# Layer 1 of a two-layer trunk: the stage from the projection to the experts in a fixed order, with a pairwise ranking of the experts

## The chip, the cores and the metric

One NeuronCore of a Trainium2 chip runs the whole program. The metric is device microseconds of one execution; the time of a kernel is the median of its runs. The profile is that of one execution, taken by the hardware profiler. TensorE (PE), VectorE (DVE), ScalarE (ACT), GpSimd (POOL) and the DMA queue of SyncE (SP) run side by side and wait for each other by semaphores; each takes its instructions in order.

## The reference

512 tokens of width 1024 pass two layers. Each layer has a mixer, a cross-attention into 256 memory tokens and a mixture of 16 experts; after each of the three the sum with the scaled input is normalised. The stage that is edited begins in the output projection `wo` of layer 1's cross-attention and ends in its experts:

```
x = layer_norm(ALPHA * x + memory_cross_attention(x, mem, xq, xkv, xo), ln2_g, ln2_b)
x = layer_norm(ALPHA * x + grouped_moe(x, router_w, router_bias, e_gate, e_up, e_down), ln3_g, ln3_b)

# grouped_moe
scores = softmax(xt @ router_w)                  # 512 x 16
biased = scores + router_bias
grouped = biased.reshape(-1, 4, 4)               # 4 groups of 4 experts
group_score = sum(top_k(grouped, 2))             # best two of each group
g_sel = argmax(group_score)                      # one group for each token
_, local_idx = top_k(in_group, 2)                # two experts of it
weights = sel / sum(sel)                         # by the scores without bias
for e in range(16):
    he = silu(xt @ w_gate[e]) * (xt @ w_up[e])
    y += combine[:, e:e+1] * (he @ w_down[e])
```

## The kernel before

The tokens lie in four tiles `X[0]` to `X[3]` of 128 rows. Every matmul of the trunk is done in three (`mm3`, L281): both operands are split into a high and a low part. All weights come as one stream `W` (class `Stream`, L108) of pieces of 512 KB: SP loads a piece into a `raw` buffer (`pump`, L129), ScalarE makes its high part (`whi`, L153) and VectorE the low one (`wlo`, L156) in `prepare`; `take` gives the pieces to a matmul and splits `look` pieces further on (3, in the experts 4), `last_ahead` bounds that. `depth` pieces are loaded ahead of the one that is split (21 in the experts of layer 1, so piece i is loaded as piece i - 22 is split); before the experts `pump` loads up to 26 pieces past the split ones. A pool of 44 buffers holds pieces, split parts and other tiles.

`project_and_norm` (L388) does the projection `wo`: its first 512 columns for all tiles together (`rows_together`), then the second 512 columns tile by tile (`rows_of_tile`, 24 matmuls of 512 columns for each tile). For each tile VectorE adds the residual (L339), takes the statistics (L352, L357) and applies the norm (L381, L386), with the power on GpSimd (L346). `r.tile_in` (L868) follows for each tile: a transfer of the tile to DRAM from ScalarE's queue (L870), 8 transposes (L875), the copy of the transposes (L879, for the last half tile L877 on VectorE), the scaling by ALPHA in place and its transfer (L880, L881), and the logits of the 16 experts (16 matmuls of 16 columns, L885; evacuated by L886). The steps of the tiles are advanced one behind the other; the logits of tile t follow the matmuls of tile t + 1. After the last tile's logits `route` (L890) chooses for all 512 tokens at once: maximum, exponential, sum, division, bias (L901 to L908), then the two best of each group by maximum, comparison and removal, and the best group (L914 to L935), giving a mask `mk` of 0 and 1. `cnt` (L941, L942) counts with small matmuls which place of an expert's list a token has (`pos`, L943).

`moe` (L1051) makes the lists: `index` (L1007) compares `pos` of an expert with the slots (`one_hot`, L973), sums token numbers by matmuls (L996), converts them (`set_rows`, L1001 and L1002), and GpSimd gathers the tokens' rows from DRAM (`fetch`, L1033). `weights` (L947) and `largest` (L961) come in between. `turned(0)` transposes and splits the gathered rows (L268, L258, L259). `experts` (L1091) then runs for each expert: gate of the next expert, down, up of the next expert, 24 matmuls of 512 columns each, with 12 weight pieces; the product of gate and up is L1112, its transposes are L1121, the split of these is `hT`.

Order: outside of `tc.manual_schedule` the compiler orders the instructions of each engine by priority and readiness; inside it the instructions of TensorE, ScalarE and VectorE keep the order in which the code emits them. Before, only `experts` stood in such a block. Layer 0 runs the same functions, and fills the choosing time of TensorE with the keys of layer 1's memory (`kfill`).

## Time and profile before

| | us |
|---|---|
| median of three runs | 1307.77 |
| lowest and highest | 1305.97, 1308.52 |
| the profiled execution, own time | 1310.58 |
| its span, first to last instruction | 1308.4 |
| mean granted TensorE clock | 0.979 of full |
| share of the span busy: TensorE, VectorE, ScalarE, GpSimd | 95%, 75%, 59%, 13% |

A line of a timeline has the start in us from the span's start, the length in us, the engine, the source line, the operation, output <- input with their shapes and the number of merged instructions; in brackets stands how long the engine was idle before, and what ended that. Of merged instructions the length is that of all together. In a table of stretches each engine has its busy time and, in brackets, its instructions; then come the granted TensorE clock, the busy share of the DMA engines and what they moved in GB/s.

### The profile page before, as it was taken

How to read it: one execution, taken by the hardware profiler on the slowest of the kernel's cores; microseconds unless marked ns; L12 is line 12 of the kernel's file. 1: busy time of each engine (PE TensorE's matmuls, PEld its weight loads, DVE VectorE, ACT ScalarE, POOL GpSimd, SP SyncE). 2: the span in 40 equal slices, each digit the busy share in tenths (PEclk: the TensorE clock that was granted, in tenths of full speed). 3: DMA queues.
4: the chain of work that ended last, by engine and by line, in shares of the span. 5: the costliest groups of instructions: out<-in, count | busy, mean ns of one | idle time of the engine just before them, and what ended most of it. 6: DMA issues, size and time to landing. Idle time of an engine off the chain costs nothing. (4 is left out here: it accounts for less than half of the span.)

```text
span 1308.4 us, 18639 instructions
## 1 busy us (share of the span) xinstructions
PE 1242.6 (95%) x6680; PEld 1042.5 (80%) x6680; DVE 982.5 (75%) x1482; ACT 768.8 (59%) x1143; POOL 170.4 (13%) x171
## 2 busy tenths in 40 slices
PE   8999999999989999999997979999978999999996
PEld 6877989888888888787775968888866888888873
DVE  4785746474769999998885586738567999999975
ACT  4765613363348888878763433227226878778873
POOL 2010001000101101111011130100011111111113
PEclk9999999999999999999998999999988999999997
DMA  9113422329549999999997333105754999999993
GB/s 320 53 49 113 164 79 81 97 89 324 192 151 325 340 339 341 328 342 345 345 355 238 130 103 122 65 33 185 263 197 145 334 365 336 345 348 346 351 324 134
DMA packets 133666, 298.81 MB, mean 228 GB/s; under 512 B 13819, under 2 KB 15883, under 8 KB 133568
## 3 DMA queue, kind: packets, MB, share of 16 engines
q1 hardware_dynamic: 118528, 260.08, 55.8%
q0 software_dynamic: 12160, 27.01, 7.5%
q10 hardware_dynamic: 2880, 10.49, 2.1%
q8 instruction: 53, 0.87, 0.3%
q14 instruction: 45, 0.37, 0.1%
HBM read 287.40 MB, written 26.74 MB: 240 GB/s over the span
## 5 line engine op out<-in xcount | busy, mean ns | idle before, releaser
L156 DVE TENSOR_TENSOR wlo<-raw,whi 128x1024 fp32r<-128x1024 f32 x486 | 572.1, 1221 | 94.1 <-ACT whi L153 70.0
L153 ACT ACTIVATE whi<-raw 128x1024 fp32r<-128x1024 f32 x488 | 490.8, 1059 | 70.6 <-PE mm L283 26.3
L282 PE MATMUL mm<-whi,xgTh 128*128 128x512 f32 x512 | 207.9, 406 | 0.0
L284 PE MATMUL mm<-whi,xgTl 128*128 128x512 f32 x512 | 201.0, 393 | 0.0
L283 PE MATMUL mm<-wlo,xgTh 128*128 128x512 f32 x512 | 200.2, 391 | 0.0
L284 PEld LDWEIGHTS mm<-whi,xgTl 128*128 128x128 f32 x512 | 96.4, 188 | 21.6 <-DVE xgTl L259 0.2
L1038 POOL DMA_INDIRECT l_y<-ye,r_idx x31 | 49.8, 1606 | 473.3 <-ACT ye L1155 209.4
L283 PEld LDWEIGHTS mm<-wlo,xgTh 128*128 128x128 f32 x512 | 97.0, 189 | 18.0
L282 PEld LDWEIGHTS mm<-whi,xgTh 128*128 128x128 f32 x512 | 96.8, 189 | 17.7 <-ACT xgTh L258 0.2
L284 PE MATMUL mm<-whi,hT 128*128 128x512 f32 x256 | 103.5, 404 | 3.3 <-DVE hT L259 3.3
L282 PE MATMUL mm<-whi,hT 128*128 128x512 f32 x256 | 103.7, 405 | 1.4 <-ACT hT L258 1.4
L283 PE MATMUL mm<-wlo,hT 128*128 128x512 f32 x256 | 101.4, 396 | 0.7 <-DVE wlo L156 0.7
L258 ACT ACTIVATE xgTh<-tp 128x512 fp32r<-128x512 f32 x64 | 38.2, 602 | 67.2 <-PE tp L268 67.2
L268 PE MATMUL tp<-ident,x 128*128 128x128 f32 x384 | 58.0, 285 | 17.4 <-DMA x<-in_x_dram 6.3
L268 PEld LDWEIGHTS tp<-ident,x 128*128 128x128 f32 x384 | 48.7, 147 | 27.7 <-issue 12.2
L346 POOL TENSOR_TENSOR ln_rs<-ln_rs,half_neg 128x1 f32<-128x1 f32 x24 | 31.7, 1320 | 286.2 <-DVE ln_rs L345 286.2
L284 PEld LDWEIGHTS mm<-whi,hT 128*128 128x128 f32 x256 | 48.7, 190 | 21.2 <-DVE hT L259 11.3
L258 ACT ACTIVATE x1Th<-tp 128x256 fp32r<-128x256 f32 x32 | 12.1, 383 | 86.5 <-PE tp L268 75.9
L282 PE MATMUL mm<-x1Th,whi 128*128 128x256 f32 (+1 forms) x192 | 60.7, 321 | 0.7 <-DVE xqTl L259 0.7
L283 PE MATMUL mm<-x1Tl,whi 128*128 128x256 f32 (+1 forms) x192 | 60.9, 318 | 0.0
L284 PE MATMUL mm<-x1Th,wlo 128*128 128x256 f32 (+1 forms) x192 | 60.9, 318 | 0.0
L283 PEld LDWEIGHTS mm<-wlo,hT 128*128 128x128 f32 x256 | 48.8, 191 | 11.1 <-DVE wlo L156 1.8
(328 smaller groups left out, 2547.7 us busy)
## 6 DMA issues: line engine op xcount, KB each, us to landing
raw<-in_l_e_gate_dram SPq DMA_DIRECT2D x128, 512.0 KB, 5.5
raw<-in_l_e_up_dram SPq DMA_DIRECT2D x128, 512.0 KB, 6.6
raw<-in_l_e_down_dram SPq DMA_DIRECT2D x128, 512.0 KB, 5.6
raw<-in_l_xkv_dram SPq DMA_DIRECT2D x32, 512.0 KB, 5.4
raw<-in_l_w_in_dram SPq DMA_DIRECT2D x22, 512.0 KB, 6.4
raw<-in_l_w_out_dram SPq DMA_DIRECT2D x16, 512.0 KB, 4.2
raw<-in_l_xq_dram SPq DMA_DIRECT2D x16, 512.0 KB, 4.5
raw<-in_l_xo_dram SPq DMA_DIRECT2D x16, 512.0 KB, 3.7
```

The source lines that it names most:

```text
L153: first = act(hi, raw, AF.Copy)
L156: self.last_split = [first, eng.tensor_sub(lo, raw, hi.bitcast(F32))]
L258: act(hi, src, AF.Copy)
L268: transpose(tp[:, j], rows(c0 + j), ident)
L282: mm(ps, sh, mh, start=first, stop=False)
L283: mm(ps, sh, ml, start=False, stop=False)
L284: return mm(ps, sl, mh, start=False, stop=last)
L346: nc.gpsimd.tensor_tensor(rs[:, 1:2], rs[:, 0:1], half_neg[:, 0:1], op=ALU.pow)
L1038: return nc.gpsimd.indirect_dma_start(out=self.y_dram[:], out_offset=bass.IndirectOffsetOnAxis(ap=idx, axis=0), in_=ye, in_offset=None, bo ...
```

## The change

In layer 1 the part from the second half of the projection to the end of the experts stands in one `manual_schedule` block, so its order on TensorE, ScalarE and VectorE is the order of the code. A new function `project_and_route` writes this order: the logits of a tile stand inside the matmuls of a later tile (after the fourth of eight chunks); the scaling of a tile is put off by two tiles; the first three tiles choose their experts in one step, and then the last tile alone, its logits read from PSUM; a weight piece of the first expert is split between the two. `last_ahead` holds the splitting of the experts' weights back until then: one piece is split there and one after `weights`, where three were split during the projection before. `moe` of layer 1 makes the lists of experts 0 and 1, then the weights, then the transposes. `warm_up` issues matmuls whose result nobody reads: 8, 8 and 9.

For both layers `choose` ranks the experts of a group by comparing each with each: greater, or equal and earlier (`tri`), counted by a sum; `G` is four groups times the tiles; the mask is "fewer than two above" in the best group.

```
+WARM = (8, 8, 9)
...
-    def rows_of_tile(xT, w, n, t):
+    def rows_of_tile(xT, w, n, t, jobs={}):
...
+            if k in jobs:
+                next(jobs[k], None)
...
+    def project_and_route(xT, key, ln, r, warm):
+        end = W.span[(key, 1)][1]
+        W.last_ahead = end
+        w = W.take((key, 1))
+        tiles = [r.tile_in(t) for t in range(NT)]
+        three, one = r.choose(slice(0, NT - 1)), r.choose(slice(NT - 1, NT))
+        for t in range(NT):
+            ln.residual(t, 1, rows_of_tile(xT, w, 512, t, {SPLIT_AT: tiles[t - 2]} if t > 1 else {}))
+            if t == NT - 1:
+                next(tiles[2])
+            ln.norm(t)
+            if t > 1:
+                r.scaled(t - 2)
+            if t == 1:
+                next(tiles[0])
+            elif t == 2:
+                next(tiles[1])
+        next(tiles[2], None)
+        warm(WARM[0])
+        steps(three, 2)
+        r.scaled(2)
+        next(tiles[3])
+        W.prepare(end + 1)
+        next(tiles[3], None)
+        warm(WARM[1])
+        steps(one, 2)
+        r.scaled(3)
+        r.count()
+        W.last_ahead = 1 << 30
...
+    def warm_up(n, oh=None):
+        ps = mmt("warm")
+        x = tb.tok.rearrange("p t e c -> p (t e c)") if oh is None else oh.rearrange("p t s -> p (t s)")
+        for _ in range(n):
+            mm(ps[:, :x.shape[-1]], tb.upto, x, start=True, stop=True)
...
+        def choose(self, ts):
+            lg = self.last_lg if ts.start else self.lg[:, ts]
...
             red(mx, lg, axis=AX.X, op=ALU.max)
-            tt(lg, lg, over(mx), op=ALU.subtract)
-            ex, bi = w16("exp"), w16("biased")
-            act(ex, lg, AF.Exp)
+            tt(ex, lg, over(mx), op=ALU.subtract)
+            act(ex, ex, AF.Exp)
             red(total, ex, axis=AX.X, op=ALU.add)
             vec.reciprocal(rt, total)
             tt(bi, ex, over(rt), op=ALU.mult)
             tt(bi, bi, tb.b[:, None, :].to_broadcast(T3), op=ALU.add)
...
+            S = [128, G, 4, 4]
...
+            tt(above[:, :, :, 4:], other, own, op=ALU.is_equal)
+            tt(above[:, :, :, 4:], above[:, :, :, 4:], tb.tri[:, None].to_broadcast(S), op=ALU.mult)
+            tt(above[:, :, :, :4], other, own, op=ALU.is_gt)
+            red(flat(rank), above, axis=AX.X, op=ALU.add)
+            vec.scalar_tensor_tensor(top, rank, 1.5, bi, op0=ALU.is_lt, op1=ALU.mult)
+            red(gs.rearrange("p t g -> p (t g)"), flat(top), axis=AX.X, op=ALU.add)
             red(gm, gs, axis=AX.X, op=ALU.max)
             tt(gs, gs, bc(gm), op=ALU.is_equal)
+            tt(gs, gs, tb.desc[:, None, :4].to_broadcast([128, n, 4]), op=ALU.mult)
             red(gf, gs, axis=AX.X, op=ALU.max)
             tt(gs, gs, bc(gf), op=ALU.is_equal)
+            vec.scalar_tensor_tensor(flat(mk), flat(rank), 1.5, each, op0=ALU.is_lt, op1=ALU.mult)
...
+            for e in range(2):
+                ohs.append(r.one_hot(r.pos[:, :, e:e + 1]))
+                r.sums(ps[e][:, 0], ohs[e], tb.tok[:, :, e], 0, 2)
+                r.set_rows(r.idx[:, e:e + 1], ps[e])
+                W.after = fetch(e)
+            warm(WARM[2], ohs[1])
+            r.weights()
+            W.prepare(W.split + 1)
+            xT = turned(0)
+            for e in range(2):
+                r.sums(ps[e][:, 0], ohs[e], tb.tok[:, :, e], 2, 5)
+            r.largest()
+            for e in range(2):
+                r.set_weights(r.ws[:, e:e + 1], ps[e])
             ln = experts(r, xT, groups, fetch, turn_part, turned, keep)
...
+            rows_together(oT, W.take((p + "xo", 0)), 512, lambda t, ps: ln.residual(t, 0, ps))
+            with tc.manual_schedule(engines=THREE):
+                project_and_route(oT, p + "xo", ln, r, warm_up)
+                W.depth, W.look = MOE_DEPTH[p], MOE_LOOK
+                ln = moe(r, None, True, warm_up)
```

## Rows read from the trace of the kernel before

**Rows 1.** Page, part 1: busy time, share of the span, instructions.

```profile
PE 1242.6 (95%) x6680; PEld 1042.5 (80%) x6680; DVE 982.5 (75%) x1482; ACT 768.8 (59%) x1143; POOL 170.4 (13%) x171
```

**Rows 2.** Table of stretches, layer 0's first expert and then layer 1.

```profile
385.00:390.00 5.00, 3.63 (x19) 3.63 (x20) 4.86 (x6) 5.00 (x7) 0.00 (x0) 0.66 0.01 6
970.00:985.00 15.00, 5.02 (x46) 4.61 (x46) 9.09 (x47) 1.97 (x4) 1.69 (x2) 0.50 0.28 110
990.66:1004.37 13.71, 13.71 (x63) 11.15 (x62) 11.98 (x15) 12.33 (x15) 1.22 (x1) 0.90 0.36 101
995.00:1005.00 10.00, 10.00 (x53) 8.19 (x52) 8.53 (x13) 8.32 (x10) 1.22 (x1) 1.00 0.56 163
1020.00:1250.00 230.00, 229.78 (x1118) 187.38 (x1117) 216.06 (x235) 186.58 (x229) 33.40 (x24) 1.00 0.98 347
```

**Rows 3.** Timeline of VectorE, norm of the last tile.

```profile
963.43 0.69 DVE L339 SCALAR_TENSOR_TENSOR x<-x,mm 128x512 f32<-128x512 f32 x1 [3.30 <-PE mm L284]
...
966.92 1.28 DVE L386 SCALAR_TENSOR_TENSOR x<-x,ln_rs,ln_b 128x1024 f32<-128x1024 f32 x1 [0.44 <-POOL ln_rs L346]
```

**Rows 4.** Timeline of TensorE, logits and transposes after the projection.

```profile
963.24 1.85 PE L885 MATMUL lg<-router_w,rxT 128*128 128x16 f32 x16
964.94 1.07 PE L875 MATMUL tp<-ident,x 128*128 128x128 f32 x8
...
970.64 3.60 PE L885 MATMUL lg<-router_w,rxT 128*128 128x16 f32 x16 [1.28 <-ACT rxT L879]
```

**Rows 5.** Timeline of VectorE, the choice and the first index.

```profile
974.49 0.22 DVE L901 TENSOR_REDUCE r_max<-r_lg 128x4 f32<-128x64 f32 x1 [4.41 <-ACT r_lg L886]
...
976.34 0.22 DVE L914 TENSOR_REDUCE rg_m<-r_biased 128x16 f32<-128x64 f32 x1
976.59 0.22 DVE L915 TENSOR_TENSOR r_d<-r_biased,rg_m 128x64 f32<-128x64 f32 x1
...
978.13 0.17 DVE L924 TENSOR_TENSOR rg_gs<-rg_m,rg_m 128x16 f32<-128x16 f32 x1
...
979.59 0.22 DVE L935 TENSOR_TENSOR r_mk<-r_s,rg_gs 128x64 bf16<-128x64 f32 x1
...
980.59 1.29 DVE L973 TENSOR_TENSOR r_oh<-slot,r_pos 128x512 bf16<-128x512 f32 x2
...
982.00 0.15 DVE L1002 TENSOR_SCALAR r_idx<-r_row 128x1 int32<-128x1 f32 x1
```

**Rows 6.** Timeline of GpSimd, the gather of expert 0.

```profile
983.01 1.12 POOL L1033 DMA_INDIRECT x<-l_x,r_idx  x1 [16.13 <-DVE tokv L957]
```

**Rows 7.** Timeline of TensorE, transposes and gate of expert 0, transposes of h.

```profile
987.36 1.94 PE L268 MATMUL tp<-ident,x 128*128 128x128 f32 x8 [3.39 <-DMA x<-l_x,r_idx]
989.13 0.79 PE L282 MATMUL mm<-whi,xgTh 128*128 128x512 f32 x1
...
993.96 0.39 PE L282 MATMUL mm<-whi,xgTh 128*128 128x512 f32 x1
...
996.68 0.25 PE L996 MATMUL idx<-tokv,r_oh 128*128 128x5 bf16 x4
...
1005.98 0.60 PE L1121 MATMUL tp<-ident,h 128*128 128x128 f32 x4
```

**Rows 8.** Timeline of VectorE, second half of the gathered rows, first product.

```profile
989.97 0.69 DVE L259 TENSOR_TENSOR xgTl<-tp,xgTh 128x512 fp32r<-128x512 f32 x1 [0.16 <-ACT xgTh L258]
...
1004.37 0.68 DVE L1112 TENSOR_TENSOR h<-h,mm 128x512 f32<-128x512 f32 x1
```

**Rows 9.** Timeline of layer 0, transposes and split of expert 0's rows.

```profile
383.63 1.06 PE L268 MATMUL tp<-ident,x 128*128 128x128 f32 x8 [1.88 <-DMA x<-l_x,r_idx]
...
384.92 1.29 DVE L259 TENSOR_TENSOR xgTl<-tp,xgTh 128x512 fp32r<-128x512 f32 x2 [3.91 <-ACT xgTh L258]
```

**Rows 10.** Timeline of VectorE at the end of the experts.

```profile
1266.98 2.59 DVE L156 TENSOR_TENSOR wlo<-raw,whi 128x1024 fp32r<-128x1024 f32 x2 [0.82 <-ACT whi L153]
...
1273.35 0.69 DVE L1112 TENSOR_TENSOR h<-h,mm 128x512 f32<-128x512 f32 x1 [1.69 <-PE mm L284]
```

99 lines of the change are left out of this document (50 added, 49 removed).

## The prediction

> **What bounds the kernel now.** I read the busy line of the page first: TensorE works in 95% of the span, so a change to some 50 us in the middle can move little unless it empties a hole [rows 1]. Then the table of stretches, cut at the borders of the stage that is edited [rows 2]. It shows three regimes. From 970 to 985 TensorE works 5.02 of 15 us at a granted clock of 0.50, the 1.2 GHz level; this is the hole in which the experts are chosen. From 995 to 1005 it is full, and the DMA is not (0.56). From 1020 to 1250 TensorE (229.78 of 230), VectorE (216.06) and the DMA (0.98 of its time) are all at their limit together. So the time won in the hole must pass a second gate: the first expert, where VectorE is the tight engine, and a third: the stream of weights.
>
> The timelines of the hole give its chain. VectorE gets the last tile's second half of the projection at 963.43, after waiting 3.30 us for TensorE, and ends the tile's norm 4.77 us later, at 966.92 + 1.28 = 968.20 [rows 3]; the logits start at 970.64 and take 3.60 us at the low clock, where those of tile 1 took 1.7 [rows 4]; the choice runs on VectorE from 974.49 to 979.59 + 0.22 = 979.81, the index is ready at 982.15 [rows 5], the gather is issued at 983.01 [rows 6], and the first transpose on its rows starts at 987.36 [rows 7]. The split of these rows is finished at 989.97 + 0.69 = 990.66 [rows 8]; I call this point T.
>
> **Part 1: the order up to the last tile's norm.** The logits of tile 1, 1.70 us (963.24 to 964.94, [rows 4]), used to follow the last tile's matmuls; now they stand inside them, after the fourth of eight chunks. VectorE waits for TensorE there [rows 3], so the last tile's half ends at 963.43 + 1.70 = 965.13 and its norm, the same 4.77 us, at 969.90. I call this R. It is a loss of 1.70 us. The transposes and logits of tile 2 (some 3.3 us from 964.94 on) still fit before R. Gone from this stretch are three early splits of expert weights, on VectorE 1.2 us each, and the scaling of a tile right behind its transfer, which is put off on ScalarE by two tiles. As TensorE sets the pace here, I give both nothing; were that cover gone, the splits would be worth up to 3.6.
>
> **Part 2: two choices in place of one.** No row has the pairwise operations, so I size them by elements: 16 elements take 0.17 us and 64 take 0.22 [rows 5], 512 take 0.69 [rows 3], which is 0.153 + 0.00105 per element (1.22 for the 1024 of a split); a dependent operation follows 0.03 after the end (976.34 to 976.59 with 0.22 busy). The part from the maximum to the biased scores took 974.49 to 976.34 = 1.85 us for four tiles, with the exponential on ScalarE inside; by size I take 1.75 for three tiles, 1.55 for one. The ranking part has 12 operations. Three tiles: 3 of 192 elements, one overlapped (1.07), a sum over 384 (0.59), 3 of 48 (0.72), 5 small (1.0) = 3.4. One tile: 0.68 + 0.32 + 0.6 + 0.95 = 2.55. So three tiles end at R + 5.15. VectorE's order is now fixed: behind them stands the split of one weight piece, 1.2 us, to R + 6.3, and only then the last tile's choice, 4.1 us. Its logits are ready earlier if the clock holds: before, they began 970.64 - 968.20 = 2.4 after R; now the exponential of the three tiles, a scaling and its transfer's issue stand ahead of the copy on ScalarE, and I take 3.1, so logits of 1.7 end at R + 4.85. At the low clock (3.6) they end at R + 6.7. So the mask is complete at R + 10.4 = 980.3, against 979.81: the chain from R became 1.2 us shorter, but R is 1.7 later. For the unseen sizes: the ranking parts have 1550 elements in all, 1.6 us, so a cost of only the fixed part gives 1.6 less for both choices and twice the cost per element 1.6 more; I keep the fitted value, since the rows are tensor operations of the same engine, but keep both ends for the range.
>
> **Part 3: index and gather.** Nine of the ten counting matmuls no longer need the last mask, and weights are no longer mixed in before the positions: the one-hot of expert 0 starts 0.5 us after the mask (before: 980.59, 0.78 after). The index of expert 0 no longer stands behind the second one-hot; 1.40 in place of 1.56. Index at 982.2 against 982.15; issue and landing as before, 0.86 and 4.35 [rows 5 to 7]. Rows of expert 0 at 987.4: no change.
>
> **Part 4: the warm matmuls.** They are 8, 8 and 9, of 320 columns and 512 in the last; at 0.227 us for 512 columns at the high clock (the gate's last 12 matmuls take 993.96 to 996.68, [rows 7]) about 1.1, 1.1 and 2 us, all in waits of TensorE. Before, the clock fell to the 1.2 GHz level by 970, some 6.5 us after the last tile's matmuls, though logits and transposes ran meanwhile [rows 2, 4]; in layer 0 it fell sooner: the key matmuls end 1.88 us before 383.63, then only transposes run, and the stretch 385:390 has 0.66 [rows 2, 9]. So I trust the warm matmuls for the logits of the last tile and for the transposes of expert 0, less for the gate. With the clock held, transposes to T take 2.58 us as in layer 0 (383.63 to 384.92 + 1.29 = 386.21, [rows 9]) instead of 987.36 to 990.66 = 3.30: T is 0.7 us earlier. The gate before paid for the low clock too: its 24 matmuls went from 989.13 to 996.68 = 7.55; at the later pace, 0.227 each, they take 5.46, so 2.1 us were lost [rows 7]. The Trainium skill ("TensorE: Matmul & The Clock Gate", section "Why this matters for your kernels") advises to leave no long idle gaps between bursts so that the clock stays up; by that advice alone these 2.1 us would be won as well.
>
> **Part 5: why the gate's share is not won.** At T only two pieces of expert 0's weights are split, before three. VectorE from T = 990.66 to expert 0's product at 1004.37 had 11.98 us of work in 13.7 [rows 2, 8]. Now come one more split (1.2), the one-hot of expert 2 (0.6, before ahead of T), and the largest count and two weight sums (0.5): 14.3 in all, so the product starts 0.6 later from T and, with T 0.7 earlier, about 0.1 earlier than before. TensorE had 0.9 us of slack against it there (product done 1005.05, transposes of h at 1005.98, [rows 7, 8]), so it gains up to 0.9 for a moment and then waits for the low half of hT, which VectorE makes after the product: I let it keep 0.5. From there on the period is the same.
>
> **Part 6: the stream of weights.** A piece is loaded when the piece 22 before it is split. 27 pieces lie ready at the gate instead of 29; the two more (524 KB each, 1.5 us at the 347 GB/s of 1020:1250) fall at 995 to 998, where the DMA is used to 0.56 [rows 2], so I cost them at nothing. If that cover were gone, 3.0 us would come at the end, where VectorE splits the last two pieces of an up matrix from 1266.98 to 1269.57 after a wait, and TensorE, done with that matrix at 1273.3, started on its last piece (6 matmuls, 1.37 us) at 1271.95: 2.4 us are left [rows 10].
>
> **Part 7: layer 0** gets the new choice for four tiles at once: by the same sizes 3.72 us against the 976.34 to 979.81 = 3.47 of the same lines in layer 1 [rows 5]; TensorE waits there 1.88 us for the gathered rows [rows 9], so this is on the path: +0.2 (-1.4 to +1.8 by the same two ends).
>
> **Sum:** -0.5 + 0.2 = -0.3 us on the profiled execution, whose span is 1308.4 and whose own time 1310.58 is 2.8 us above the median of the runs shown, 1307.77. Carried to the median: 1307.5.
>
> **Rivals.** *The clock decides, VectorE does not* (faster). If the extra VectorE work fits into TensorE's faster first expert, the 0.7 and the 2.1 us of part 4 come through whole, and with half of the early split (0.6), should it slip out of the chain: 1307.77 - 2.8 - 0.6 + 0.2 = 1304.6. For it: rows show the low clock all through the hole; TensorE, not VectorE, is the full engine in 995:1005 [rows 2]. Against it: part 5's count. This is also where the skill's advice leads.
> *The clock falls in spite of the warm matmuls and the fixed order makes everyone wait* (slower). The last logits at 3.6 us put the last choice at R + 6.7 (+0.4), transposes stay at 3.3 (+0.7), and a gate at the low clock takes TensorE's slack against the first product (+0.5): 1.6 later than in my sum, 1309.1; with the pairwise operations at their upper end (+1.6, layer 0 +1.6) 1312.3. It decides from the point where the logits end after R + 6.3, when VectorE would be free.
> *The stream sets the end*: the hole shrinks, but the last pieces come no earlier; TensorE waits for them. As 2.4 us are left there, this gives 1307.8, or up to 1309 if part 6's cover is gone.
> *The change doesn't do what it says*: the three early choices cannot start before VectorE has finished the last tile's norm, so "first" buys only their 5.15 us beside the logits; that is in my sum.
>
> **How the numbers follow.** A measurement of this kernel tells about 0.2% (2.6 us) from no change. Forecast 0.44 and stream 0.07 are within 0.2%. Clock decides: 0.28, all of it faster. Slow rival: 0.21; its plain price stays within 0.2%, and I give two thirds, 0.14, to the bounds that carry it past 1310.4, and 0.07 to no change. Range: the forecast with both ends of the pairwise cost is 1304.3 to 1310.7; with the faster case and the plain slow one inside it is 1304.0 to 1310.8. Faster 0.28, same 0.58, slower 0.14.
>
> **What would show it.** Right: the norm of the last tile ends near 970 in the new trace, the last mask near 980, the gather is issued within 0.7 us of 983; the stretch from T to the first product is longer than before and without waits of VectorE, while TensorE shows a wait for h of about a microsecond after the first gate. Wrong: a wait of VectorE for the last tile's logits (the slow rival), a first product 2 us or more earlier (the fast one), a longer wait of ScalarE for the last pieces (the stream). I would be most wrong if the pairwise operations cost other than by their elements, or if the order before the hole moves TensorE's work differently than by 1.70.

## The result and the profile after

The changed kernel is slower: 1316.28 us (1314.87 to 1318.12) against 1307.35 of the kernel before in the same series, a ratio of 1.0070 with a 95% interval of 1.0052 to 1.0087, or +9.2 us. A second series of it gave +4.1 us (ratio 1.0031, interval 1.0011 to 1.0051). Both lie on the side that had a chance of 0.14, and the first median lies outside the range of 1304.0 to 1310.8. The profiled execution of the changed kernel took 1315.8 us, its span is 1314.1.

The busy line of the page says little: 5.3 us more of TensorE in a span that is 5.7 us longer than that of [rows 1].

```profile
PE 1247.9 (95%) x6705; PEld 1043.5 (79%) x6705; DVE 986.0 (75%) x1486; ACT 771.1 (59%) x1144; POOL 170.3 (13%) x171
```

The table of stretches of the changed kernel is to be read beside [rows 2]. Its columns are the stretch and its length, the busy time of TensorE, its weight loads, VectorE, ScalarE and GpSimd, then the granted clock, the DMA's share and GB/s. The layer-1 stage lies some 3.5 us later here, so 975:990 stands for 970:985, and 994.14:1007.93 (point T to the first product) for 990.66:1004.37.

```profile
385.00:390.00 5.00, 3.32 (x18) 3.08 (x17) 4.01 (x5) 4.78 (x7) 0.00 (x0) 0.56 0.06 20
975.00:990.00 15.00, 9.54 (x50) 6.39 (x51) 11.79 (x49) 4.45 (x7) 2.13 (x2) 0.54 0.44 150
994.14:1007.93 13.79, 13.79 (x70) 11.27 (x69) 13.72 (x21) 13.38 (x16) 1.22 (x1) 1.00 0.52 159
1020.00:1250.00 230.00, 228.51 (x1109) 185.69 (x1108) 213.33 (x235) 185.23 (x226) 36.05 (x26) 1.00 0.96 336
```

The hole in which experts are chosen is fuller (TensorE 9.54 of 15 us instead of 5.02, more than half of it warm matmuls), and the clock is at its upper level from T on. But from T to the first product VectorE works 13.72 of 13.79 us, so nothing got shorter there; and the stream in 1020:1250 is slower, 336 GB/s instead of 347.

The timeline of VectorE in the changed kernel, from the second half of the last tile to the first product of layer 1, is to be read beside [rows 3, 5, 8]:

```profile
968.74 0.69 DVE L342 SCALAR_TENSOR_TENSOR x<-x,mm 128x512 f32<-128x512 f32 x1 [3.44 <-PE mm L285]
...
972.22 1.29 DVE L389 SCALAR_TENSOR_TENSOR x<-x,ln_rs,ln_b 128x1024 f32<-128x1024 f32 x1 [0.44 <-POOL ln_rs L349]
...
975.12 0.36 DVE L973 TENSOR_TENSOR above<-r_biased 128x192 f32<-128x192 f32 x1
...
978.25 0.21 DVE L990 SCALAR_TENSOR_TENSOR r_mk<-r_rank,rg_gs 128x48 bf16<-128x48 f32 x1
978.38 1.22 DVE L157 TENSOR_TENSOR wlo<-raw,whi 128x1024 fp32r<-128x1024 f32 x1
980.26 0.17 DVE L961 TENSOR_REDUCE r_max<-lg 128x1 f32<-128x16 f32 x1 [0.67 <-PE lg L937]
...
984.11 0.17 DVE L990 SCALAR_TENSOR_TENSOR r_mk<-r_rank,rg_gs 128x16 bf16<-128x16 f32 x1
...
984.80 0.69 DVE L1028 TENSOR_TENSOR r_oh<-slot,r_pos 128x512 bf16<-128x512 f32 x1
...
1004.52 3.49 DVE L157 TENSOR_TENSOR wlo<-raw,whi 128x1024 fp32r<-128x1024 f32 x3
1007.93 0.68 DVE L1185 TENSOR_TENSOR h<-h,mm 128x512 f32<-128x512 f32 x1
```

The norm of the last tile ends at 973.51; three tiles have chosen 4.95 us later, at 978.46. The first product follows VectorE's weight splits without a gap, while the gate and up matmuls that it needs are over at 1006.0: VectorE, and not TensorE, sets its time. The new wait of VectorE in the choice, 0.67 us ahead of 980.26, is for the last tile's logits. The timeline of TensorE has them, in the place of the last row of [rows 4], at the low clock all the same:

```profile
976.63 3.60 PE L937 MATMUL lg<-router_w,rxT 128*128 128x16 f32 x16 [1.97 <-ACT rxT L931]
```

At the end of layer 1 (VectorE's products, then ScalarE's splits of weights, both of the changed kernel; [rows 10]) the experts run out of weights:

```profile
1245.61 0.68 DVE L1185 TENSOR_TENSOR h<-h,mm 128x512 f32<-128x512 f32 x1
1265.31 0.68 DVE L1185 TENSOR_TENSOR h<-h,mm 128x512 f32<-128x512 f32 x1
1280.92 0.68 DVE L1185 TENSOR_TENSOR h<-h,mm 128x512 f32<-128x512 f32 x1
```

```profile
1271.41 2.23 ACT L154 ACTIVATE whi<-raw 128x1024 fp32r<-128x1024 f32 x2 [1.75 <-DMA raw<-in_l_e_down_dram]
```

Two products lie 19.70 us apart where the same two lay 17.99 apart before; over the last four distances this execution lost 4.3 us, from the first product to the last 4.0, and ScalarE waits 1.75 us for a transfer. So against the execution that the prediction was made from: layer 0's first product is 1.9 us later (405.69 to 403.76), up to layer 1's stage this grows to 3.5, the stage from the projection to the first product adds 0.1, and the experts behind it 4.0. Behind the last product 1.9 us come back, which leaves the 5.7 us between the spans.

### The profile page after: what moved, and what is told of

Read it like the earlier page. It is cut to its first block, busy times and chain, and to the rows that moved or that the text cites. A ratio compares the mean times of both kernels' runs of the same rounds, so it can differ in the third digit from the quotient of the medians.

```text
span 1314.1 us, 18689 instructions
## 1 busy us (share of the span) xinstructions
PE 1247.9 (95%) x6705; PEld 1043.5 (79%) x6705; DVE 986.0 (75%) x1486; ACT 771.1 (59%) x1144; POOL 170.3 (13%) x171
## 5 line engine op out<-in xcount | busy, mean ns | idle before, releaser
L154 ACT ACTIVATE whi<-raw 128x1024 fp32r<-128x1024 f32 x488 | 492.8, 1060 | 66.8 <-PE mm L284 22.9
L285 PEld LDWEIGHTS mm<-whi,hT 128*128 128x128 f32 x256 | 48.3, 189 | 22.5 <-DVE hT L260 12.8
```

Of the source, the lines that this page charges most:

```text
L154: first = act(hi, raw, AF.Copy)
L285: return mm(ps, sl, mh, start=False, stop=last)
```

## The experiments

All series against the kernel before in the same rounds; the difference is the ratio less one, times 1306 us.

| kernel | median us | before | ratio, 95% interval | difference us |
|---|---|---|---|---|
| e1, ranking alone | 1311.24 | 1305.22 | 1.0046, 1.0027 to 1.0065 | +6.0 (3.5 to 8.5) |
| e1b, the same again | 1310.01 | 1305.90 | 1.0028, 1.0013 to 1.0043 | +3.7 (1.7 to 5.6) |
| e3, old ranking in layer 0 | 1309.82 | 1305.22 | 1.0029, 1.0010 to 1.0048 | +3.8 (1.3 to 6.3) |
| e6, the same, 28 pieces | 1311.28 | 1306.82 | 1.0039, 1.0016 to 1.0061 | +5.1 (2.1 to 8.0) |
| e2, changed, 28 pieces | 1313.47 | 1305.22 | 1.0062, 1.0042 to 1.0083 | +8.1 (5.5 to 10.8) |
| e4, changed, early splits | 1317.29 | 1305.22 | 1.0092, 1.0063 to 1.0122 | +12.0 (8.2 to 15.9) |
| a1, changed again | 1310.47 | 1306.82 | 1.0031, 1.0011 to 1.0051 | +4.1 (1.4 to 6.7) |
| e5, changed, layer 0 filled | 1313.11 | 1306.82 | 1.0049, 1.0026 to 1.0071 | +6.4 (3.4 to 9.3) |
| b2, before itself | 1304.33 | 1305.90 | 0.9984, 0.9969 to 0.9999 | -2.1 (-4.0 to -0.1) |
| f, before, thin stream | 1305.93 | 1305.90 | 1.0006, 0.9992 to 1.0019 | +0.8 (-1.0 to 2.5) |
| f, changed, thin stream | 1310.41 | 1305.90 | 1.0033, 1.0015 to 1.0052 | +4.3 (2.0 to 6.8) |
| k1, before, scratch moved | 1306.86 | 1307.20 | 1.0002, 0.9982 to 1.0022 | +0.3 (-2.4 to 2.9) |
| k4, before, table added | 1308.71 | 1307.20 | 1.0012, 0.9991 to 1.0032 | +1.6 (-1.2 to 4.2) |
| k2, ranking mended | 1308.90 | 1307.20 | 1.0020, 1.0002 to 1.0038 | +2.6 (0.3 to 5.0) |
| k3, changed, mended | 1310.08 | 1307.20 | 1.0028, 1.0008 to 1.0048 | +3.7 (1.0 to 6.3) |
| v1, before, logits first | 1304.01 | 1305.65 | 0.9993, 0.9971 to 1.0014 | -0.9 (-3.8 to 1.8) |
| v2, the same, filled | 1303.46 | 1305.65 | 0.9984, 0.9960 to 1.0007 | -2.1 (-5.2 to 0.9) |

### Which half costs: the ranking, or layer 1's order

My theory after the result was that the stream of weights, which I had costed at nothing, took some 4 us, and layer 0 some 3. **e1** is the kernel before with the new ranking in both layers and nothing else:

```diff
-            red(m1, bi4, axis=AX.X, op=ALU.max)
-            tt(d4, bi4, each(m1), op=ALU.is_equal)
...
-            tt(grouped(mk), s14, each(gs), op=ALU.mult)
+            tt(above[:, :, :, 4:], other, own, op=ALU.is_equal)
...
+            vec.scalar_tensor_tensor(flat(mk), flat(rank), 1.5, each, op0=ALU.is_lt, op1=ALU.mult)
```

> The kernel before with one edit: the ranking by pairwise comparisons in both layers, everything else (the planner's order, the choice of the four tiles together, the weight pieces) as before. In layer 0 the changed kernel started the choice 0.42 us later, had its mask 0.50 us later (375.58 to 376.08) and the gather of the first expert 0.66 us later, and its first product came 1.93 us later, its last expert's 3.03 us later. Theory A (the ranking itself sets layer 0 back, through the gather and the low clock behind it): layer 0's first product again about 1.9 us later, at the start of layer 1's stage about 3 us behind, and the whole about 1310 to 1312. Theory B (layer 0's 3 us are a matter of the single execution, not of the ranking, which the prediction costed at 0.2): the whole within 1307 to 1308.5, with the first product of layer 0 at most 0.7 us later.

Measured: 1311.24 us, in theory A's range, but 6.0 us above the kernel before in the same rounds, which is more than theory A meant. In its trace the first product of layer 0 is 5.17 us later, for the most part through a low clock (0.73 in 370:375, 0.50 in 390:395); but at layer 1's first product it stands only 0.06 us behind the trace of the kernel before. That contradiction was the first sign that the execution the prediction rests on was itself a slow one. **e3** takes the ranking back in layer 0 only:

```diff
+            if not self.one:
+                red(m1, bi4, axis=AX.X, op=ALU.max)
...
+                tt(grouped(mk), s14, each(gs), op=ALU.mult)
+                return
```

> The changed kernel with the old ranking (22 operations) back in layer 0; layer 1 is as in the changed kernel. Theory A (layer 0's share is due to the ranking there): layer 0's first product comes at the old time (403.8, not 405.7), layer 1's stage starts 3.4 us earlier than in the changed kernel, and the whole is 3 to 3.5 us less, about 1313. Theory B (layer 0's share has nothing to do with the ranking): the whole stays at 1315.3 to 1317.3. Should the whole fall by more than 4 us, layer 0's lateness also bears on layer 1's stream.

Measured: +3.8 us, lower than theory A had it (1309.8 instead of 1313). e3 is not layer 1's part alone: the small table of the new ranking, which is computed at the start of the kernel, is still in it, and its first product of layer 0 is at 404.82, not at 403.8. Each half is slower by itself, and neither in the way that I expected; nor do they add up, as 6.0 and 3.8 (later 3.7 and, with 28 pieces, 5.1) stand against 9.2 and 4.1 for the whole.

### Not the two missing pieces, and not the stream

**e2** asks for two more pieces ahead of the gate, **e4** lets three pieces be split early again, **e6** is e2's edit on e3:

```diff
-GATE_DEPTH = {"l0_": 24, "l1_": 26}
+GATE_DEPTH = {"l0_": 24, "l1_": 28}
```

> The changed kernel with one number changed: layer 1's limit of weight pieces asked for ahead of the gate is 28 instead of 26, so that 29 pieces are on their way at the gate as in the kernel before (the changed kernel had 27). The last four experts of layer 1 lost 0.55, 2.25, 3.96 and 4.29 us against the ones before them, with TensorE and VectorE waiting for weights. Theory A (the two missing pieces are what runs out at the end: the stream sets the end): the last four experts keep the distance of the others, the whole falls by 3 to 4.3 us, to 1312 to 1313. Theory B (the stream runs slower for another reason, or as it happens in the execution): the whole stays within 1 us of the changed kernel, 1315.3 to 1317.3.

> The kernel with layer 1's part alone (the old ranking in layer 0), with layer 1's limit at the gate at 28 instead of 26, so that 29 pieces are on their way as in the kernel before. Layer 1's part alone gave 1309.8 against 1305.2 of the kernel before, though in its profiled execution layer 1's stage and experts stood where those of the kernel before did. Theory A (the two missing pieces make the stream run out in some executions, and that is layer 1's share): 1305 to 1307, with no executions above 1311. Theory B (layer 1's share comes from the fixed order or elsewhere): 1309 to 1311, as without it.

```diff
-        W.last_ahead = end
...
-        W.prepare(end + 1)
...
-            W.prepare(W.split + 1)
```

> The changed kernel without its three holds on the early splitting of weights: three pieces of the experts' weights are split during the projection again, as in the kernel before, so that 29 pieces are on their way at the gate with the limit left at 26. The splits stand on VectorE and ScalarE between the steps of the choice: three pieces, some 1.1 us of VectorE each. Theory A (the stream's deficit of two pieces costs the end): the last four experts keep the distance of the others and the whole falls by up to 4 us, less up to 2 us where the splits delay the choice: 1312 to 1315. Theory B (the deficit is not the cause): no gain at the end, and the splits in the choice's way make it up to 2 us longer: 1316 to 1318.5.

e2 was at +8.1 us. In its profiled execution the last experts keep their distance, but that is the fastest of its executions, so it decides nothing. e6 says more: with 28 pieces e3 is no faster (5.1 us above the kernel before, 3.8 without), and its last experts lost 1.5 us all the same. e4 is worst: the splits stand in front of the last tile, from the first split of the attention's output to that tile's residual it takes 66.8 us instead of 58.6, and the first product of layer 1 comes 6.3 us later than in the kernel before. That is theory B for e4 and e6, while e2 (1313.47) lies between its two theories: the two pieces are not shown to matter, and holding the splits back was worth its price.

The trace of the weight queue tells when the end loses time. The last group of four "up" pieces is issued 247.0 to 251.3 us after layer 1's first product in the executions that lose nothing, and 252.6 to 255.7 after it in those that lose 0.8 to 4.0 us; beyond about 252 the loss follows roughly one to one. Each execution has slow patches of its own. The fixed order lost at the end in five of eight traces with whole weights, the old order in three of ten. A count made afterwards divides them better: all eight that lose have the new ranking or its table, and of the six that have neither (k1, v1 and v2 among them) none loses. What causes that is not known. **f** lightens the stream: half of the gate weights of 15 experts are not loaded.

```diff
-                self.last = nc.sync.dma_start(raw, ap)
+                if self.loaded in self.thin:
+                    self.last = nc.sync.dma_start(raw[:, :1], ap[:, :1])
+                else:
+                    self.last = nc.sync.dma_start(raw, ap)
```

> The kernel before with half of the bytes of the gate weights of layer 1's experts 1 to 15 (only the first of the two blocks of each piece is loaded, and split twice): 60 of the pieces of layer 1 are 256 KB instead of 512 KB, a sixth of the stream, some 45 us of it at 1.5 us a piece; every instruction of TensorE, VectorE and ScalarE is the same. So layer 1's weights can no longer run out. Theory A (in the kernel before the stream has a small reserve and runs out in few executions): within 1.5 us of the kernel before, with fewer executions above 1308. Theory B (layer 1's experts are paced by the stream in this kernel too): 3 us or more below.

> The changed kernel with the same halved gate weights. In four of seven traces with the fixed order the last experts of layer 1 lost 1.5 to 4.3 us to weights that had not come, in none of three with the old order. Theory A (the stream running out at the end of layer 1 is most of what the change costs): 3 to 4 us below the changed kernel, and within 2 us of the kernel before with the same halving. Theory B (what the change costs lies ahead of the experts): still 3 us or more above the kernel before with the halving.

+0.8 and +4.3 us: with a sixth less to load the changed kernel still stands as far above as in its second series. Theory B: what the change costs in this pair lies ahead of the experts of layer 1, or in layer 0. Their traces agree: at layer 1's first product the changed one is 5.7 us later (2.6 of it a low clock in the stage, this time in the fixed order), at the last product 4.7. The end is not rid of waits, though: from the first to the last product it took 271.3 and 270.2 us instead of 269.0, with waits of ScalarE of up to 2.8 and 2.9 us ahead of weight splits; so the pair shows only that the changed kernel lost no more there.

### A second look at both kernels, and the yardstick

> The changed kernel once more, on the chip of the next three, to have a second trace of it. The two halves added gave +6.0 us (the ranking alone in both layers, 1305.2 to 1311.2) and +4.6 us (layer 1's part alone, 1309.8). Theory A (the halves add up and the loss at the end of the stream is a property of the kernel): 1314 to 1317, the last four experts of layer 1 again lose 3 to 5 us against the first twelve, and the granted clock around layer 0's gate is low for two stretches (385 to 392) again. Theory B (the loss at the end of the stream happened to that one execution): the last four experts keep their distance and the profiled execution is at 1310 to 1312.

> The kernel before once more, for a second trace: its 21 executions beside the first four experiments were 1302.4 to 1309.7, median 1305.2, while the one that the prediction was made from had 1310.6. Theory A (the difference between executions of one and the same kernel lies in the low-clock stretches and in the store that the last tile's scaling waits for in layer 0, near 366): this execution is at 1303 to 1308 and is shorter in the stretch 690 to 950 or in the tail, and the distances of layer 1's experts are the same 18.04 us as before. Theory B (it lies in the weight stream of the experts): the experts of layer 0, 405 to 690, are where it is shorter by 3 us or more.

a1: +4.1 us; it lost 2.3 us at the end, and around layer 0's gate the clock was low for one stretch, not two, so neither theory holds whole. b1 (1306.36) told most. Its theory A holds, but the stage, which the theory does not name, differs as much as the tail. From the second half of the last tile's residual to layer 1's first product it takes 39.12 us, where [rows 3, 8] have 1004.37 - 963.43 = 40.94; and from the last product to the end 33.1 us instead of 35.05. These two places are 3.8 of the 4.2 us between the two executions. **b2** gives the same once more, and says what a series is worth:

> The kernel before, timed against itself in the same rounds as the next three: what two series of one kernel differ by. The changed kernel's two series stood 9 us and 3.7 us above the kernel before, which is more than either interval allows for. Theory A (a series carries its own shift of some us, whatever the kernel): the ratio is away from 1.000 by 0.002 or more. Theory B (the differences belong to the kernels): the ratio is within 0.001 of 1.000, 1305 to 1308 us.

0.9984, between the two theories: 2.1 us below itself, so differences of 2 us between series of this kernel are not to be trusted. Its rows (VectorE, the same two instructions as in [rows 3, 8]), and behind them those of k3, which is the changed kernel without the two side effects in layer 0 that the next section shows:

```profile
961.81 0.69 DVE L339 SCALAR_TENSOR_TENSOR x<-x,mm 128x512 f32<-128x512 f32 x1 [3.30 <-PE mm L284]
1000.58 0.68 DVE L1112 TENSOR_TENSOR h<-h,mm 128x512 f32<-128x512 f32 x1
```

```profile
966.68 0.69 DVE L342 SCALAR_TENSOR_TENSOR x<-x,mm 128x512 f32<-128x512 f32 x1 [3.45 <-PE mm L285]
1005.61 0.68 DVE L1188 TENSOR_TENSOR h<-h,mm 128x512 f32<-128x512 f32 x1
```

38.77 and 38.93 us. The stretch 950:1020 shows the difference between the two kinds of execution of one order, here that of the prediction, b2 and the changed kernel, in this order:

```profile
950.00:1020.00 70.00, 56.72 (x323) 47.98 (x322) 51.14 (x101) 35.38 (x49) 10.55 (x8) 0.83 0.53 188
```

```profile
950.00:1020.00 70.00, 57.62 (x330) 48.80 (x329) 53.24 (x103) 37.25 (x49) 11.82 (x9) 0.85 0.57 201
```

```profile
950.00:1020.00 70.00, 61.16 (x348) 48.52 (x347) 54.71 (x108) 35.23 (x49) 8.03 (x7) 0.90 0.57 194
```

In all traces of the old order, a mean clock of 0.85 goes with 38.7 to 39.1 us (six of them) and 0.83 with 40.5 to 41.0 (five). The fixed order has 0.90 and 38.9 to 39.3 us in six of nine; e5 has 0.88 and 40.1, f's changed kernel, with the same warm matmuls, 0.83 and 41.3, and e4 has its splits ahead of this stretch. Without e4 the mean is 39.5 us, in the old order 39.7. So the fixed order mostly does what the old one does in half of its executions, and pays 1.85 us for it ahead of this stretch: from the first split of the attention's output to this residual it takes 58.6 us instead of 56.8, in each of its traces but e4's.

Why it gains nothing against an undisturbed execution stands in the stretch from T to the first product, here of b2:

```profile
988.13:1000.58 12.45, 12.45 (x63) 10.21 (x62) 11.89 (x14) 12.32 (x15) 1.23 (x1) 1.00 0.33 105
```

There the old order has the upper clock all along and needs 12.45 us, where the execution of the prediction needed 13.71 at a clock of 0.90. The changed kernel comes to T sooner, by 0.72 us in the transposes and 0.2 in the wait for the rows, but then needs 13.79 us, because its VectorE has 13.72 us of work there instead of 11.89.

### Layer 0: the clock, a table and a buffer

**e5** fills the wait of TensorE in layer 0:

```diff
             self.set_weights(self.ws[:, s], ps)
+            if es == [0]:
+                for _ in range(FILL):
+                    mm(fill, self.tb.upto, ohs[0].rearrange("p t s -> p (t s)"), start=True, stop=True)
```

> The changed kernel with twelve matmuls more in layer 0, 128x512, whose result nobody reads, behind the sums of the first expert and ahead of its transposes: they fill the 2.4 us in which TensorE waited for the gathered rows; the seven key matmuls that stood there go behind the transposes, where TensorE waited 1.7 us for a weight split. Theory A (the ranking in layer 0 costs what it costs through TensorE's idle time and the low clock that follows it): the granted clock stays at 1.00 from 380 to 395, the key matmuls run at 0.12 us each instead of 0.21, layer 0's first product comes 1.5 to 2.5 us earlier than in the changed kernel, and the whole is 2 to 5 us below the changed kernel. Theory B (layer 0's share is the later gather, or something that lies behind the experts' stream): the clock may hold, but the whole is within 1 us of the changed kernel.

The clock held (table of stretches of e5; the clock is third from the end):

```profile
380.00:395.00 15.00, 13.12 (x102) 10.54 (x103) 10.45 (x26) 7.07 (x12) 2.15 (x2) 1.00 0.11 31
```

From the gather to the first product it took 24.62 us, where executions with one low stretch have 24.3 to 24.6 and those with two 25.2 to 26.1. So a held clock is worth a microsecond there against two low stretches and nothing against one, and the whole was +6.4 us: theory B. And the low clock around the gate is no matter of the ranking: b1, with the old one, has two low stretches, a1 with the new one has one. This theory fell.

What the traces with the new ranking have in common lies further ahead. **At the start**, VectorE stands at the new table until GpSimd has written the column numbers; the first split of the input waits behind it. First the kernel before (b2), then the changed kernel:

```profile
6.22 0.42 DVE L259 TENSOR_TENSOR xTl<-tp,xTh 128x256 fp32r<-128x256 f32 x1 [5.27 <-ACT xTh L258]
```

```profile
7.10 0.17 DVE L888 TENSOR_TENSOR tri<-desc 128x16 f32<-128x16 f32 x1 [6.15 <-POOL desc L885]
7.19 0.42 DVE L260 TENSOR_TENSOR xTl<-tp,xTh 128x256 fp32r<-128x256 f32 x1
```

**In layer 0**, ScalarE scales the last tile in place and must wait until that tile is stored; the half of it that the logits need is copied behind that. The timeline of ScalarE in b2 and in the changed kernel:

```profile
363.21 1.06 ACT L880 ACTIVATE x<-x 128x1024 f32<-128x1024 f32 x1 [1.69 <-DMA l_x<-x]
...
364.44 0.59 ACT L879 ACTIVATE rxT<-tp 128x512 f32<-128x512 f32 x1
```

```profile
366.05 1.06 ACT L917 ACTIVATE x<-x 128x1024 f32<-128x1024 f32 x1 [3.29 <-DMA l_x<-x]
...
367.27 0.59 ACT L931 ACTIVATE rxT<-tp 128x512 f32<-128x512 f32 x1
```

The wait is 1.6 to 1.9 us in seven traces with the old ranking there, 2.8 to 5.4 in the eight with the new one as the change has it. The ranking runs after it, so it can act only through what is planned ahead: its scratch `above` comes out of the 44 buffers that the weight pieces go round in. **k1** moves one scratch tile of the old ranking there, **k4** adds the table alone, **k2** and **k3** mend both in e1 and in the changed kernel:

```diff
-            d, s1 = w16("d"), w16("s1")
+            d, s1 = unit(T3, name="d"), w16("s1")
```

> The kernel before with one word changed: a scratch tile of the old ranking comes out of the 44 buffers that the weight pieces go round in, as the new ranking's scratch does; every instruction and its order is the same. In the seven traces with the old ranking in layer 0 ScalarE waits 1.6 to 1.9 us for the store of the last tile (at 364 to 365), in the eight with the new one 2.8 to 5.4 us, and a weight piece is issued 0.3 to 1.7 us ahead of that store where it followed it by 0.03 us. Theory A (the scratch tile moves the rotation of the buffers by one, one piece no longer waits and goes ahead of the store): the wait is 2.8 us or more here too, the logits of layer 0's last tile start up to 2 us later, in some executions the clock falls behind them, and the whole is 1 to 3 us above the kernel before. Theory B (the later store has another cause in the new ranking): wait 1.6 to 1.9 us and the time of the kernel before within 0.7 us.

In k1 two pieces of "up" are issued from 358.06 on (the second at 359.71), ahead of the store at 359.74; in b2 the first of them follows the store (359.08) at 359.12. Timelines of the weight queue and of ScalarE, in turn, of b2 and then of k1:

```profile
359.12 0.38 SPq L133 DMA_DIRECT2D raw<-in_l_e_up_dram  x1
```

```profile
359.08 0.38 ACTq L870 DMA_DIRECT2D l_x<-x  x1
```

```profile
358.06 2.01 SPq L133 DMA_DIRECT2D raw<-in_l_e_up_dram  x2
```

```profile
359.74 0.38 ACTq L870 DMA_DIRECT2D l_x<-x  x1
...
367.98 1.06 ACT L880 ACTIVATE x<-x 128x1024 f32<-128x1024 f32 x1 [5.81 <-DMA l_x<-x]
```

So the mechanism is shown, with no other instruction changed: one buffer more in the rotation, and the wait is 5.81 us; the logits began at 369.84, and the first product of layer 0 came 4.5 us later than in b2. The traces have two grades of it. With one piece ahead of the store, by 0.3 to 0.8 us (the changed kernel in both traces, e2, e4 and f's), the wait is 2.8 to 3.6 us, and the logits begin at 368.4 to 369.3, about as in e3, e6 and k4, which have the table and the short wait (368.9 to 369.1). With two ahead (k1, e1, e1b, e5) it is 4.6 to 5.8, the logits begin at 369.6 to 369.8, the granted clock falls to 0.60 to 0.78 in 370:375, and the gather follows the logits by 12.8 to 14.6 us instead of 11.2 to 11.6. The order of issue is the plan's own: both traces of e1 have two pieces ahead, both of the changed kernel one. So e1 is not a clean half of the change, nor e5, whose gather came late in spite of its held clock at the gate, a clean test of the fill. But k1's series is +0.3 us (-2.4 to 2.9). What it costs the whole is therefore not shown, and by this interval at most 3 us.

```diff
+            vec.tensor_tensor(self.tri, d[:, None, :].to_broadcast([128, 4, 4]),
+                              d[:, :, None].to_broadcast([128, 4, 4]), op=ALU.is_gt)
```

> The kernel before with one instruction more: the small table of the new ranking, computed on VectorE at the start, which nothing reads. In all traces that have it VectorE stands at it until 7.08, when GpSimd has the column numbers, and the first split of the input ends 0.85 to 1.2 us later than in the four traces without it (7.17 against 5.99 to 6.34). Theory A (that wait is on the path and goes through to the end): first split at 7.17, layer 0's logits 0.8 to 1.3 us later than 367.8, the whole 0.8 to 1.3 us above the kernel before. Theory B (it is swallowed by some later wait): the logits at 367.2 to 368.1 as before.

VectorE in k4:

```profile
7.09 0.17 DVE L846 TENSOR_TENSOR tri<-desc 128x16 f32<-128x16 f32 x1 [6.14 <-POOL desc L843]
7.19 0.42 DVE L259 TENSOR_TENSOR xTl<-tp,xTh 128x256 fp32r<-128x256 f32 x1
```

The logits of layer 0 began at 369.01, and at 369.06 and 368.86 in e3 and e6, which have the table beside the old ranking; the eight traces without the table have 367.0 to 368.2, k1 apart. Theory A: about 1 us goes through 360 us of kernel unabsorbed. The time, +1.6 us, agrees and cannot tell it from nothing.

```diff
-            above = unit([128, NT * 4, 4, 8], name="above")[:, :G]
+            above = sm([128, NT * 4, 4, 8], BF, name="r_above")[:, :G]
...
+                tc.add_manual_dep(tri.ins, peak.ins.name, ORDER, reason="not ahead of the first splits")
```

> The ranking alone in both layers, once more. It stood 6.0 us above the kernel before (1311.2 to 1305.2), though in its trace the ranking itself made the first gather of layer 0 only 0.25 us later, counted from the last tile's logits, and layer 1's experts stood where those of the kernel before did. Theory A (the ranking costs 0.25 us and 0 to 0.4 us, as its rows say, and the 6 us were a low-clock stretch at 370 behind a late store, 3.3 us, and chance): 1306 to 1309. Theory B (there is something in it that the trace did not show): again 5 to 7 us above the kernel before.

> The ranking alone in both layers, mended at two places: its scratch has a buffer of its own (in bf16, 1 KB, so that it fits), and its table is computed at the first choice and not at the start. The ranking alone stood 6.0 and 4.1 us above the kernel before. Theory A (the table's wait at the start, 1 us, and the piece ahead of the store, 2 us and at times a low clock, are what it costs): first split at 6.0 to 6.3, store wait 1.6 to 1.9 us, and the whole within 1.5 us of the kernel before. Theory B (the ranking itself costs, for instance through the clock behind the gather): still 3 us or more above.

> The changed kernel mended at the same two places; layer 1 as in the changed kernel. Theory A: what is left is layer 1's part: the last tile's residual 1.85 us later, from there to the first expert 39.0 to 39.3 us where the kernel before has 38.8 to 39.1 in three executions of four (40.9 in the one that the prediction was made from); so 2 us above the kernel before, 1.5 to 3 us below the changed kernel. Theory B (the two places are not what it costs): as the changed kernel, 3.7 us or more above the kernel before.

e1b gave +3.7 us, between its two theories, with the store's wait at 5.39. Mended, the ranking stands at +2.6, again between them: its first split is at 5.96 and its logits at 367.91, but the store's wait was 2.35, between the two groups. k3 is at +3.7, with a wait of 1.62 and the logits at 368.22. The traces went as theory A says, the times did not: k3's is theory B's (3.7 or more). They moved the right way, by 1 to 3 us for the ranking and by 0.4 us for the change against its second series, within what a series shifts by itself. So the table and the wait are shown in layer 0's rows, and not that ridding the kernel of them makes it faster.

### A faster version?

**v1** is the kernel before with the scaling of layer 0's last tile put behind the exponentials, **v2** has e5's fill as well:

```diff
-            act(X[t], X[t], AF.Copy, scale=ALPHA)
-            nc.scalar.dma_start(self.y_dram[tok(t)], X[t])
...
+            self.evac = act(ex, lg, AF.Exp)
+            self.scaled(NT - 1)
...
+                tc.add_manual_dep(first.ins, self.evac.ins.name, ORDER, reason="logits go first")
```

> The kernel before with one order changed: the scaling of the last tile in layer 0, which waits for that tile's store, goes behind the exponentials of the choice on ScalarE instead of ahead of the tile's last transposed half. ScalarE then no longer waits 1.7 us ahead of the logits, and TensorE has the logits eight key matmuls, 1.0 us, earlier. Theory A (the store's wait stands on layer 0's path): logits at 366.5 to 367 instead of 367.2 to 368.1, the first gather 1 to 1.5 us earlier, and the whole 0.5 to 2 us below the kernel before. Theory B (layer 0's experts take their time from the weight stream): the first product comes earlier, and the last expert of layer 0 does not; the whole within 0.7 us.

> The same, with ten matmuls more in layer 0 whose result nobody reads, in the place where TensorE waits for the first gathered rows. With twelve of them in the changed kernel the granted clock stayed at 1.00 around the gate, and from the gather to the first product it took 24.6 us, where eleven traces without them have 24.3 to 24.6 (clock low for one stretch) or 25.2 to 26.1 (for two). Theory A: 24.3 to 24.6 us from the gather to the first product, and the whole 0.5 to 1.5 us below the kernel without them. Theory B (absorbed by the weight stream): no difference to it beyond 0.7 us.

v1's first gather is issued at 378.67, that of the kernel before at 378.37 in b2 and at 379.0 to 379.3 in three other traces: the planner put the logits earlier (367.03), but eight key matmuls, and not one, stand between their two halves, so at most 0.6 us was won there. v2's clock stayed at 1.00 around the gate, with 24.44 us from the gather to the first product. The series are -0.9 and -2.1 us, both intervals with zero inside. They are below the changed kernel, but not shown to be below the kernel before.

## Why the prediction was wrong

**Right.** Part 1: the last tile's residual 1.85 us later, forecast 1.70. (It reads [rows 4] rightly: in the kernel before the logits of a tile followed the matmuls of the tile two further on, not of the next one, as the description of that kernel has it.) Part 2: three tiles at R + 4.95, forecast 5.15, so sizing the pairwise operations by elements held (192 elements took 0.36 us, by the formula 0.35). Part 3: the one-hot 0.5 us after the mask. Part 4: the transposes to T took 2.58 us and the gate 5.6, forecast 2.58 and 5.46. Part 5: VectorE is the bound up to the first product, 13.72 of 13.79 us, and so what TensorE gained there did not come through. Part 7's own number: the gather follows the logits of layer 0 by 11.46 us instead of 11.22, +0.24, forecast +0.2. Part 6's pieces: e6 speaks for costing them at nothing.

**The step that failed first: the yardstick under parts 4 and 5.** I set a loss of 1.70 against gains in the stage, the 2.1 us of a gate at the low clock among them, and kept "-0.5" as their sum. Then I carried that to the median by taking off the 2.8 us by which the profiled execution stood above it. Those 2.8 us were partly the same time: b1 and b2 show that the execution was slow in this stage by 1.8 to 2.2 us, and by 1.9 in its tail. From the residual to the first product my parts add up to 1004.27 - 965.13 = 39.1 us, and the changed kernel has 39.19; but an undisturbed execution of the kernel before has 38.8 to 39.1. So the gain was no gain, and the loss of 1.85 stayed. That 39.1 came out so well is in part luck: the rows of expert 0 came 18.04 us after R and not 17.5, mostly because the last choice waited for its logits, and from T to the product it took 13.79 us and not 14.3.

**Part 4, the clock.** The logits of the last tile ran at the low level (3.60 us) though eight warm matmuls stood ahead of them, and the choice waited 0.67 us: the slow rival's condition. The gate ran at the upper level, where I trusted it less. The Trainium skill ("TensorE: Matmul & The Clock Gate", section "Why this matters for your kernels") advises against long idle gaps between bursts. The traces agree on the clock in six of nine, 0.90 instead of 0.83 and 0.85 over 950:1020; they do not on the time, 39.19 us against b2's 38.77, because VectorE was full there.

**Part 7 left two things out.** I sized the new operations of layer 0 and not what comes with them. The table: an instruction of 0.17 us with a wait for GpSimd, ahead of VectorE's first split, some 1.0 us on the path. I had put down each wait that the change adds in the hole and none at the start of the kernel. The scratch: one buffer out of a rotation moves every weight piece behind it; ScalarE then waits 1 to 4 us longer for a store in layer 0. k1 shows the wait, not its price.

**Where the time went.** Four traces each of the two kernels (before, b1, b2 and f's; changed, a1, e2 and f's, so one of each with the halved weights and e2 with 28 pieces) give mean distances. They are an estimate, as traces of one kernel differ by 1 to 7 us at these places.

| stretch | forecast us | mean of the traces us |
|---|---|---|
| start to layer 0's first product (part 7) | +0.2 | +1.8 |
| to the last tile's residual in layer 1 (part 1) | +1.7 | +1.6 |
| to layer 1's first product (parts 2 to 5) | -1.8 | +0.3 |
| to layer 1's last product (rest of part 5, part 6) | -0.4 | +1.2 |

The sums are -0.3 and +4.9. The largest miss is the stage's gain that was none, then layer 0, where rows show 1.0 us for the table and 0.25 for the ranking, and the experts of layer 1 with the end of the stream. The rival "the stream sets the end" had 1307.8 to 1309 and was undersized where it acted: 4.0 us in the first profiled execution. But it acts by execution, not by the two pieces. What stays open: why k3, without the table at the start and without the longer wait, still stands 3.7 us above the kernel before; why the first series stood 5 us above the second, of which the stream's end (4.0 and 2.3 us in their two traces) is some; and whether the change makes slow patches at the end likelier.

## What to carry to other kernels

Before crediting a change with time that a profile shows as lost, look at a second execution: what only that execution lost, the change can't win, and subtracting the distance to the median afterwards counts it twice. Of every instruction that a change adds, also of constants at the start and scratch tiles, ask what is queued behind it on its engine and whose buffer it takes: here, in the rows of layer 0, a table of 0.17 us and a tile of 2 KB per partition did more than the operations that they serve. And a held clock is worth only what the tightest other engine lets through.

## What the runs showed of the hardware

The granted clock differs between executions of one program at the same place: in layer 1's stage of the old order its mean over 950:1020 is 0.83 or 0.85, with 40.5 to 41.0 or 38.7 to 39.1 us up to the first product, and around layer 0's gate the stretch 385:390 has 0.50 to 0.94 in the eighteen traces without a fill, 1.00 in the two with one (e5, v2). A store of 512 KB that has one weight piece issued just ahead of it holds ScalarE for 2.8 to 3.6 us, with two pieces ahead for 4.6 to 5.8, where it held it for 1.6 to 2.4 with none. And one series of a kernel against itself came out 2.1 us off, with an interval that excludes zero.
